# A two-layer decoder trunk: the second layer's output projection as seven half-size products inside one attention loop, split weights kept in DRAM, silu computed from tanh

## The chip, the cores and the metric

The kernel runs on one core of a Trainium2 chip. A core has five engines that run side by side, each with its own instruction queue: PE (TensorE, matrix products into PSUM), DVE (VectorE), ACT (ScalarE), POOL (GpSimd) and SP (SyncE, which here only issues DMA transfers). The metric is the device time of one execution in microseconds; lower is better.

## The reference

The input is `x` of 1024 tokens by 1024 channels, float32. Layer A is a chunked gated MLP. Layer B is sliding-window attention over a shared K/V. What matters here is layer B:

```python
q, z = jnp.split(h @ w_in, 2, axis=-1)            # (1024, 1024) each
...
logits = jnp.einsum('btkgd,bskd->bkgts', qb, kb) + alibi   # blocks of 128 tokens, window 128
...
y = out * jax.nn.silu(z)
return y @ w_out                                   # (1024, 1024) @ (1024, 1024)
```

There are 16 query heads of 64 channels on 4 K/V heads. The layer's result is rms-normalised, multiplied by a gain and added to the residual stream. The inputs of the products are float32.

## The kernel before

**Products.** Every float32 operand is split into a high part in the `fp32r` format and the rest (`split`, lines 104-110: ACT makes the high part, DVE the rest), and a product is three matmuls, high by high, high by low, low by high (`mm3`, lines 168-171). One matmul of 128 x 128 stationary values moves 512 columns.

**Layer A** (lines 298-930) already uses seven products for eight in its large matrix products, and is not touched. It ends at about 650 us.

**Layer B, first stage** (lines 1261-1276): `q_phase`, `kv_phase` and `z_phase` of the first 512 tokens (h = 0), while `chain_a` and `norm_h1` finish layer A's second half beside them, one generator step at a time. The weights come in tiles of 128 x 1024 (0.5 MB) in the order of `Weights.order` (line 120): 8 tiles of q, 4 of k/v, 8 of z, then 4, 8 and 8 again for the second 512 tokens, then 8 of the output projection. For each tile `wload` issues one transfer on SP into one of three `raw` buffers, and `split` or `split_scaled` writes the pair (`whi`, `wlo`, two buffers each). `wnext` hands out a pair and lets `ahead` split the next one and load one two further on. So each of the 20 tiles of q, k/v and z is read and split twice.

**Layer B, attention.** A `Unit` is one block of 128 tokens (b = 0 to 7) for one half of the heads (p = 0, 1). Its parts: `scores(0)` and `scores(1)` (PE 8 small matmuls each; DVE merges the window and finds the maximum; ACT takes EXP with the sum), `normalise` (DVE), `transposes` (PE 8, ACT two copies, POOL two triangular selections), `values` (PE, then ACT copy, DVE add, DVE product with the gate z, and the split of the result into the place of q). `attn` (lines 1163-1187) runs the 8 units of one half of the tokens as a software pipeline, unit i's scores beside unit i-1's transposes and unit i-2's values, in 10 rounds, and between these parts it takes steps of `fill`, a generator of other products: in the first loop k/v, q and half of z of the second tokens, in the second the rest of z and the output projection. A step is 6 matmuls of 512 columns, or about as much. Both loops run through to their ends one after the other (lines 1278-1289).

**Layer B, output.** `out_b0` (the first 512 tokens) holds four token tiles in PSUM for each half of the output columns (gd = 0, 1) and takes 8 k-tiles; `out_b1` does the second 512 tokens with split weights of a whole half in `big`, one token tile after the other, with `final` (sum of squares, power on POOL, two DVE passes, two stores) for each tile. `wo_b[gd, cp]` is the block of 256 rows (cp) and 512 columns (gd) of `w_out`.

**silu** is an ACT copy out of PSUM for each bank and one ACT SILU over two tiles (`z_phase`, lines 1010-1016).

**Order.** The program is written in Python and put in order by a scheduler that keeps each engine's instructions mostly as written and may move some by modelled times. PSUM has eight banks, four of tag `mm` and four of tag `s`.

## Time and profile before

| | |
|---|---|
| Three runs | 1056.62, 1056.23, 1053.37 us; median 1056.23 |
| The profiled execution | 1056.17 us, span 1054.5 us |
| Mean granted TensorE clock | 0.996 |
| HBM read, written | 125.28 MB, 31.46 MB |
| First attention score | about 768 us |
| Last matmul starts | 1047.77 us |

Times inside the span are in us from its start. "PE busy" is the union of the matmuls' durations, and a matmul's duration (0.39 us for 512 columns) is longer than the distance to the next one, so short gaps don't show in it. "PEld" is the loading of stationary values. A group's row gives line, engine, operation, tiles written and read, shapes and count; then busy us and mean ns; then the engine's idle time before it and what ended that. In the table by windows a row gives the stretch, its length, the busy times of PE, PEld, DVE, ACT and POOL with counts, the granted clock, the DMA share and GB/s.

### The profile page before, as it was taken

Reading aid. Unit: us, or ns where it says so; the run is one execution under the profiler, and the core shown is the slowest. Engines: PE = TensorE matmul, PEld = TensorE weight load, DVE = VectorE, ACT = ScalarE, POOL = GpSimd, SP = SyncE. Lnnn points to the kernel's source line nnn. Section 1 sums busy time; section 2 is a strip of 40 time slices with the busy share of each in tenths; the row PEclk is TensorE's granted clock in tenths of the full one; section 3 lists DMA queues with packets and bytes.
Section 4 is the critical chain, followed back from the end, with each engine's and each line's share of the span. In section 5 each row is a group of like instructions: output and inputs, shape, how many; then the busy total and the mean of one; then the engine's idle time right before and its main releaser. Section 6 shows DMA issues by size and latency. Waiting matters only on the chain.

```text
span 1054.5 us, 13950 instructions
## 1 busy us (share of the span) xinstructions
PE 1038.2 (98%) x5106; PEld 856.0 (81%) x5106; DVE 738.4 (70%) x1259; ACT 588.1 (56%) x1012; POOL 186.9 (18%) x153
## 2 busy tenths in 40 slices
PE   9999999999999999999999999999999999989997
PEld 7888888888888888888888888888898777867676
DVE  6987466867767768678596587764258885668763
ACT  6584443555565555555444474654467776686531
POOL 0000003254343542540200000100001011011120
PEclk9999999999999999999999999999999999999899
DMA  8777252334333433337997543632322122212363
GB/s 306 266 271 285 100 180 83 123 112 136 120 115 115 151 105 135 110 131 279 327 342 271 190 148 95 214 106 80 100 80 62 51 70 80 81 40 81 100 216 123
DMA packets 81508, 157.64 MB, mean 149 GB/s; under 512 B 5920, under 2 KB 33440, under 8 KB 81440
## 3 DMA queue, kind: packets, MB, share of 16 engines
q1 hardware_dynamic: 76928, 148.08, 41.1%
q10 hardware_dynamic: 4512, 8.68, 2.3%
q8 instruction: 40, 0.66, 0.2%
q14 instruction: 28, 0.23, 0.1%
HBM read 125.28 MB, written 31.46 MB: 149 GB/s over the span
## 4 chain that ended last, share of the span: by engine, by line
PE 83%; DVE 6%; ACT 5%; DMA 3%; issue 2%; POOL 1%; SPq 0%; DVEq 0%; POOLq 0%; ACTq 0%
PE ub L169 6%; PE ub L171 6%; PE ub L170 6%; PE ob L169 5%; PE qz L169 5%; PE ob L171 5%; PE ob L170 5%; PE qz L171 4%; PE qz L170 4%; PE uc L170 3%; PE uc L169 3%; PE uc L171 3%; PE sp L624 3%; PE oc L169 2%; PE oc L171 2%; PE oc L170 2%
## 5 line engine op out<-in xcount | busy, mean ns | idle before, releaser
L169 PE MATMUL qz<-n_hi,whi 128*128 128x512 f32 x256 | 101.6, 397 | 1.0 <-DVE q_lo L1004 0.8
L110 DVE SCALAR_TENSOR_TENSOR wlo<-raw_w,gn,whi 128x512 fp32r<-128x512 f32 x80 | 58.3, 759 | 61.3 <-ACT whi L109 61.1
L171 PE MATMUL qz<-n_hi,wlo 128*128 128x512 f32 x256 | 100.0, 391 | 0.3 <-DVE wlo L110 0.3
L170 PE MATMUL qz<-n_lo,whi 128*128 128x512 f32 x256 | 99.9, 390 | 0.0
L109 ACT ACTIVATE whi<-raw_w,gn 128x512 fp32r<-128x512 f32 x80 | 54.4, 715 | 53.6 <-PE qz L170 33.4
L1110 ACT ACTIVATE pr<-pr,mx 128x129 f32<-128x129 f32 x128 | 50.3, 395 | 38.3 <-DVE mx L1106 38.1
L169 PEld LDWEIGHTS qz<-n_hi,whi 128*128 128x128 f32 x256 | 48.1, 188 | 15.7 <-issue 6.2
L105 ACT ACTIVATE uzhilo_g<-f 128x1024 fp32r<-128x1024 f32 x31 | 32.9, 1061 | 49.5 <-PE uc L171 43.5
L171 PEld LDWEIGHTS qz<-n_hi,wlo 128*128 128x128 f32 x256 | 48.0, 188 | 11.1 <-DVE wlo L110 0.7
L170 PEld LDWEIGHTS qz<-n_lo,whi 128*128 128x128 f32 x256 | 48.1, 188 | 9.2
L106 DVE TENSOR_TENSOR uzhilo_g<-f,uzhilo_g 128x1024 fp32r<-128x1024 f32 x31 | 38.6, 1246 | 19.9 <-ACT uzhilo_g L105 19.9
L209 ACT ACTIVATE uz_slots<-ub 128x512 f32<-128x512 f32 x48 | 28.3, 590 | 42.4 <-PE ub L171 39.1
L169 PE MATMUL ub<-T,whi_g 128*128 128x512 f32 x128 | 50.7, 396 | 0.0
L169 PE MATMUL ub<-T,uzhilo_g 128*128 128x512 f32 x128 | 50.5, 395 | 0.0
L171 PE MATMUL ub<-T,wlo_g 128*128 128x512 f32 x128 | 49.9, 390 | 0.0
L171 PE MATMUL ub<-T,uzhilo_g 128*128 128x512 f32 x128 | 49.9, 390 | 0.0
L170 PE MATMUL ub<-T,whi_g 128*128 128x512 f32 x128 | 49.9, 389 | 0.0
L170 PE MATMUL ub<-T,uzhilo_g 128*128 128x512 f32 x128 | 49.8, 389 | 0.0
L169 PE MATMUL uc<-T,uzhilo_g 128*128 128x512 f32 x124 | 48.9, 395 | 0.0
L170 PE MATMUL uc<-T,uzhilo_g 128*128 128x512 f32 x124 | 48.3, 390 | 0.0
L171 PE MATMUL uc<-T,uzhilo_g 128*128 128x512 f32 x124 | 48.3, 389 | 0.0
L105 ACT ACTIVATE whi_g<-raw_uz 128x1024 fp32r<-128x1024 f32 (+1 forms) x31 | 26.5, 854 | 37.0 <-PE ua L170 14.5
(337 smaller groups left out, 3103.4 us busy)
## 6 DMA issues: line engine op xcount, KB each, us to landing
raw_uz<-in_wuz_in_dram SPq DMA_DIRECT2D x32, 512.0 KB, 3.5
raw_w<-in_wqz_dram SPq DMA_DIRECT2D x32, 512.0 KB, 3.5
td<-uz_slots SPq DMA_DIRECT2D x56, 256.0 KB, 2.1
orawP2a<-td SPq DMA_DIRECT2D x28, 512.0 KB, 4.1
raw<-in_wv_in_dram SPq DMA_DIRECT2D x17, 512.0 KB, 4.9
vg<-vd SPq DMA_DIRECT2D x8, 1024.0 KB, 5.4
orawP2b<-in_wo_a_dram SPq DMA_DIRECT2D x16, 512.0 KB, 8.2
vraw<-in_wv_in_dram SPq DMA_DIRECT2D x13, 512.0 KB, 5.2
```

The lines of the kernel that those rows point to most:

```text
L105: nc.scalar.activation(hi, src, AF.Copy)
L106: nc.vector.tensor_tensor(lo, src, hi.bitcast(F32), ALU.subtract)
L109: nc.scalar.activation(hi, src, AF.Copy, scale=g)
L110: nc.vector.scalar_tensor_tensor(lo, src, g, hi.bitcast(F32), ALU.mult, ALU.subtract)
L169: nc.tensor.matmul(out, lhsT=a_hi, rhs=b_hi, start=start, stop=False, skip_group_check=True)
L170: nc.tensor.matmul(out, lhsT=a_hi, rhs=b_lo, start=False, stop=False, skip_group_check=True)
L171: nc.tensor.matmul(out, lhsT=a_lo, rhs=b_hi, start=False, stop=stop, skip_group_check=True)
L209: nc.scalar.activation(out, a, AF.Copy)
L624: nc.tensor.matmul(psv[:, n], lhsT=d["vg"][:, 4 * j + n, i * P:(i + 1) * P], rhs=d["wc"], start=True, stop=True)
L1110: nc.scalar.activation(pr[:, i], pr[:, i], AF.Exp, bias=mx[:, i:i + 1], scale=-1.0, accum_out=dn[:, i:i + 1])
```

## The change

Write the gated attention output as A (1024 x 1024) and `w_out` as B, both cut in four. The output's four quarters were eight products of half size. Now they are seven, with sums on both sides (a Strassen-Winograd scheme):

- *Sums of B* (`presum`): per 512-column piece four loads, four additions or subtractions on POOL and four stores to DRAM (`sd[1]` to `sd[4]`), one generator step at a time beside q, k/v and z of the first tokens.
- *Sums of A* are made in `Unit.values`: results of the first tokens are stored to DRAM as well (`yd`), read again (`y_again`) for the units of the second tokens, and added on POOL (the last unit's on DVE); the sums' splits go into places of q0 and q1 that are free by then.
- *Three products in the loop* (`Out.early`): two accumulate in one bank set to the first quarter of the output, the third uses a sum. *Four products after it* (`Out.late`), each 4 token tiles x 4 k-tiles, with the additions between quarters on DVE and POOL, and `final` for each tile in the last two.
- *Kept weights*: when one of the first 20 tiles is split, its pair is stored to DRAM; the next 20 entries of the order read the pairs back (two transfers of 0.5 MB) instead of loading and splitting. In that stretch the pairs rotate through three places, the third made of two `raw` buffers, and are read two ahead.
- *One loop* over the 16 units with a written order of parts and filling (`ORDER`), the steps dealt out by round: 88 over the first 14 rounds, then 4 in each of the last 4. `held` chains the DVE and ACT instructions of the attention's parts in program order. `normalise` works on four heads at a time.
- *silu from tanh*: z (1 + tanh(z/2)) is twice silu(z); ACT takes TANH out of PSUM, DVE adds one and multiplies by PSUM, and the factor 0.5 goes into the copy after the transposes.

The core of the diff:

```diff
     def split(self, i):
...
-                hi = wpool.tile([P, 1024], F32R, tag="whi", name=f"whi{n}")
-                lo = wpool.tile([P, 1024], F32R, tag="wlo", name=f"wlo{n}")
+                hi, lo = (w_ring.take if 20 <= n < 40 else w_pair)(f"w{n}")
+                self.done.append((hi, lo))
+                if kind in self.kept:
+                    for t, src in zip((hi, lo), self.kept[kind]):
+                        nc.sync.dma_start(out=t.bitcast(F32), in_=src)
+                    continue
...
+                self.kept[kind] = [dram.tile([P, 1024], F32, name=f"kept{n}_{i}") for i in range(2)]
+                for t, dst in zip((hi, lo), self.kept[kind]):
+                    nc.sync.dma_start(out=dst, in_=t.bitcast(F32))
...
         def ahead(self):
-            self.split(self.at)
+            self.split(self.at + (20 <= self.at < 39))
             self.load(self.at + 2)
...
-            zt = z[m // 4]
-            nc.scalar.activation(zt[:, m % 4], ps, AF.Copy)
-            if m % 2 == 1:
-                zs = zt[:, m % 4 - 1:m % 4 + 1]
-                nc.scalar.activation(zs, zs, AF.Silu)
+            zt = z[m // 4][:, m % 4]
+            nc.scalar.activation(zt, ps, AF.Tanh, scale=0.5)
+            nc.vector.scalar_tensor_tensor(zt, zt, 1.0, ps, ALU.add, ALU.mult)
...
+            if b < 4:
+                hi, lo = (by_head(w)[:, 2 * p:2 * p + 2, t] for w in q)
+                split(hi, lo, yt.rearrange("p (m g) t -> p m g t", m=2))
+                nc.sync.dma_start(out=yd[p][t].rearrange("p (a t) -> p a t", a=4), in_=yt)
+            elif p == 0:
+                d = y_again(0, t)
+                add(mixed(d), yt, mixed(d), ALU.subtract, nc.gpsimd)
+                put(q, 0, d)
+            else:
+                hi, lo = (by_head(w)[:, 2:4, t] for w in q)
+                split(hi, lo, yt.rearrange("p (m g) t -> p m g t", m=2))
+                e = z[0][:, :, bs_]
+                eng = nc.gpsimd if t < 3 else nc.vector
+                add(e, yt, e, ALU.subtract, eng)
+                add(yt, e, mixed(y_again(0, t)), ALU.add, eng)
+                hi, lo = (by_head(w)[:, 0:2, t] for w in q0)
+                split(hi, lo, yt.rearrange("p (m g) t -> p m g t", m=2))
...
+    ORDER = "0F1FvtnmFF"
...
+    def presum():
+        for u in range(2):
+            for j in range(2):
+                cs = slice(j * 512, j * 512 + 512)
+                two = [bp.tile([P, 1088], F32, tag="pr", name=f"presum{u}{j}{i}", bufs=2) for i in range(2)]
+                a11, a21, a22, a12 = (two[i][:, k * 512:k * 512 + 512] for i in range(2) for k in range(2))
+                for t, (gd, cp) in ((a21, (1, u)), (a22, (1, 2 + u)), (a11, (0, u)), (a12, (0, 2 + u))):
+                    load(t, wo_b[gd, cp][:, cs])
+                yield from range(4)
+                made = ((1, a22, a21, a22, ALU.add), (3, a21, a11, a21, ALU.subtract),
+                        (2, a11, a22, a11, ALU.subtract), (4, a12, a12, a11, ALU.subtract))
+                for i, t, l, r, op in made:
+                    add(t, l, r, op, nc.gpsimd)
+                    yield
+                yield from range(3)
+                for i, t, *_ in made:
+                    nc.sync.dma_start(out=sd[i][u][:, cs], in_=t)
+                yield from range(7)
...
+        def late(self):
...
+            ps = [bank("mm", f"oe{t}") for t in range(4)]
+            for t in range(4):
+                for m in range(4):
+                    self.mm(ps[t], q0, 0, t, m, self.w6, m == 0, m == 3)
+                operand(q0, 1, t, t7[:, :, t * P:(t + 1) * P])
+                add(m1[t], m1[t], ps[t], ALU.add)
+                add(m5[t], m5[t], m1[t], ALU.add, nc.gpsimd)
...
+            ps = [bank("mm", f"og{t}") for t in range(4)]
+            for t in range(4):
+                for m in range(4):
+                    self.mm(ps[t], q1, 1, t, m, w3, m == 0, m == 3)
+                c = yo[t][:, 0:512]
+                add(c, m5[t], ps[t], ALU.add)
+                sumsq(ss[1][:, 0, t:t + 1], c, f"c12_{t}")
+                add(c, c, gp[:, 0:512], ALU.mult)
+                final(1, t, [c, yo[t][:, right]], ss[1])
...
-    main = q_phase(0, n0, q0)
+    main = q_phase(0, n0, q0, 0, 4)
+    sums = presum()
     step(main, main)
     for _ in main:
         step(side)
+        step(sums)
...
-    fill = chain(kv_phase(1, n1), q_phase(1, n1, q1), z_phase(1, n1, z1, 0, 4))
-    attn(0, q0, z0, fill, 64)
+    last = Out(q0, q1, gp, z1)
+    fill = chain(kv_phase(1, n1), q_phase(1, n1, q1, 0), z_phase(1, n1, z1, 0, 4), q_phase(1, n1, q1, 4),
+                 z_phase(1, n1, z1, 4, 8), last.early())
+    units = [Unit(4 * h + b, p, q, z) for h, q, z in ((0, q0, z0), (1, q1, z1)) for p in range(2) for b in range(4)]
+    attn(units, fill, [int(88 * (i + 1) / 14) for i in range(14)] + [92, 96, 100, 104])
     drain(fill)
-
-    def tail():
...
-    fill = chain(z_phase(1, n1, z1, 4, 8), tail())
-    attn(1, q1, z1, fill, 48, 2)
-    drain(fill)
+    last.late_weights()
+    last.late()
```

More of the change, by code (lines that the diff above doesn't have):

```diff
@@ L1164, in attn, with more @@
+    def attn(units, fill, by):
         taken = [0, 0]
[L1165 to L1169 removed]
+        def more(i, k):
+            lo, hi = by[i - 1] if i else 0, by[i]
+            while taken[1] < lo + (hi - lo) * (k + 1) // 4:
                 taken[1] += 1
                 step(fill)
[L1173 removed]
@@ new lines, in attn @@
+            live, mid, old = i < len(units), 0 <= i - 1 < len(units), 0 <= i - 2
+            f = iter(range(4))
+            for what in ORDER:
+                if what == "F":
+                    held(more, i, next(f))
+                elif what == "0" and live:
+                    held(units[i].scores, 0)
+                elif what == "1" and live:
+                    held(units[i].scores, 1)
+                elif what == "v" and old:
+                    held(units[i - 2].values)
+                elif what == "t" and mid:
+                    held(units[i - 1].transposes)
+                elif what == "n" and live:
+                    held(units[i].normalise, 0)
+                elif what == "m" and live:
+                    held(units[i].normalise, 1)
@@ new lines, in tile_yoco, with held @@
+    PINS, UP = (), ("DVE", "Activation")
+    ORDER = "0F1FvtnmFF"
+    behind = {}
+    def held(what, *args):
+        start = len(nc.cur_bb.bb.instructions)
+        what(*args)
+        for ins in list(nc.cur_bb.bb.instructions)[start:]:
+            e = str(ins.engine).split('.')[-1]
+            if e in PINS or what.__name__ != "more" and e in UP:
+                if e in behind:
+                    tc.add_manual_dep(ins, behind[e], mybir.DependencyInfo(
+                        mybir.DependencyClass.NoSync, mybir.DependencyReason.DATA), reason="held")
+                behind[e] = ins.name
```

233 lines of the change are left out of this document (131 added, 102 removed).

## The prediction, as it was put on record

> **What bounds the kernel now.** I read the page first, then the table by windows, then the groups by line, then the chain that ended last. On the page the profiled execution has this span and these shares:
>
> ```profile
> span 1054.5 us, 13950 instructions
> PE 1038.2 (98%) x5106; PEld 856.0 (81%) x5106; DVE 738.4 (70%) x1259; ACT 588.1 (56%) x1012; POOL 186.9 (18%) x153
> DMA  8777252334333433337997543632322122212363
> ```
>
> TensorE is busy almost throughout, DVE and ACT are not, and the transfers are light behind the middle of the span. Up to about 650 us (layer A) the change touches nothing. The windows of layer B, with two stretches of layer A for the rate of the transfers:
>
> ```profile
> 520.00:540.00 20.00, 20.00 (x89) 16.54 (x89) 18.37 (x17) 8.94 (x10) 0.00 (x0) 1.00 1.05 387
> 0.00:50.00 50.00, 48.17 (x209) 39.12 (x210) 40.35 (x46) 31.72 (x43) 1.42 (x6) 1.00 0.82 289
> 650.00:700.00 50.00, 49.69 (x221) 40.79 (x220) 33.87 (x49) 27.92 (x47) 3.82 (x3) 1.00 0.52 177
> 700.00:768.00 68.00, 68.00 (x363) 58.71 (x363) 29.45 (x43) 31.92 (x52) 0.00 (x0) 1.00 0.29 93
> 768.00:860.00 92.00, 91.09 (x562) 74.91 (x561) 72.42 (x213) 64.42 (x177) 10.92 (x10) 1.00 0.21 66
> 860.00:1048.00 188.00, 181.93 (x969) 142.23 (x967) 122.27 (x320) 108.03 (x270) 28.37 (x27) 0.98 0.30 100
> ```
>
> The columns are PE, PEld, DVE, ACT and POOL busy, granted clock, DMA share and GB/s. From 650 to 768 us (q, k/v and z of the first half) PE is full and the transfers run at 93 to 177 GB/s. From 768 to 1048 us (attention and output projection) PE has gaps, and the clock falls to 0.98 in the mean.
>
> A busy PE hides gaps shorter than a matmul, so I count that last stage. The spacing of back-to-back 512-column matmuls comes from twelve of them, the first and the last here; the price of the attention's parts from merged pieces of the chain; the counts from groups by line between 767.8 and 1048 us:
>
> ```profile
> 1045.27 0.39 PE L169 MATMUL ob<-wob_hi,q_hi 128*128 128x512 f32 x1
> ...
> 1047.77 0.39 PE L171 MATMUL ob<-wob_hi,q_lo 128*128 128x512 f32 x1
> ```
>
> ```profile
> 784.84 0.87 PE pt L1123 x8
> 785.71 0.87 PE s L1092 x8
> 857.94 1.45 PE o L1152 x16
> 985.12 0.43 PE ob L171
> ```
>
> ```profile
> L169 PE MATMUL qz<-n_hi,whi 128*128 128x512 f32 x128 | 51.8, 405 | 1.0 <-DVE q_lo L1004 0.8
> L169 PE MATMUL ob<-whi,q_hi 128*128 128x512 f32 x64 | 26.8, 419 | 0.1
> L169 PE MATMUL ob<-wob_hi,q_hi 128*128 128x512 f32 x64 | 25.1, 393 | 0.0
> L169 PE MATMUL pv<-whi,n_hi 128*128 128x256 f32 x32 | 9.1, 286 | 0.0
> L169 PE MATMUL pk<-n_hi,whi 128*128 128x512 f32 x16 | 6.5, 404 | 0.0
> ```
>
> Spacing: 2.50 us over 11 steps, 0.227 us. Each group stands for three (lines 169 to 171). So q and z: 384 x 0.227 = 87.2; output projection, 3 x (64 + 64) = 384: 87.2; k: 48 x 0.227 = 10.9; v at half the columns, 96 x 0.114 = 10.9; sixteen attention units at 2 x 0.87 (scores) + 0.87 (transposes) + 1.45 (values) = 4.06: 65.0. Sum 261 us of work in 280 us. **About 19 us are lost here**, of which some 3.5 are the clock: matmuls 0.43 us apart near 985 us, and 188 x 0.02 = 3.8. The rest are waits at the ends of the two attention loops and between: the chain runs there over ACT, DVE and POOL.
>
> **The change, part by part.**
>
> *Seven products for eight.* A product of half size is 4 token tiles x 4 k-tiles x 3 = 48 matmuls; eight were 384, seven are 336. Removed: 48 x 0.227 = **10.9 us** of PE work, in the stage where PE is the bound. No attention, q, k, v or z matmul changes.
>
> *One loop and a fixed order.* 18 rounds instead of 20, no emptied loop between, and 88 of the 104 filling steps spread over the first 14 rounds: 6.3 steps x 6 matmuls x 0.227 = 8.6 us of filling beside 4.06 of attention, 12.6 us a round. Values wait for what was transposed one round before. What the other engines must do in that round:
>
> ```profile
> L1106 DVE CUSTOM_DVE_ANT_0 pr<-s,bias,snk 128x128 f32<-128x128 f32 x128 | 39.0, 349 | 1.5
> L110 DVE SCALAR_TENSOR_TENSOR wlo<-raw_w,gn,whi 128x512 fp32r<-128x512 f32 x38 | 28.1, 770 | 18.0 <-ACT whi L109 18.0
> L1110 ACT ACTIVATE pr<-pr,mx 128x129 f32<-128x129 f32 x128 | 50.3, 395 | 38.3 <-DVE mx L1106 38.1
> L109 ACT ACTIVATE whi<-raw_w,gn 128x512 fp32r<-128x512 f32 x38 | 25.6, 712 | 3.0 <-PE pv L171 1.1 <-ACT pr L1110 1.0 <-ACT pc L1125 0.6
> L1110 ACT ACT_TABLE_LOAD x4 | 5.1, 1283 | 0.0
> L1016 ACT ACT_TABLE_LOAD x3 | 3.8, 1283 | 0.1
> ```
>
> Reading split weights back takes the splits out of the loop: 28 us off DVE, 26 off ACT, of the 195 and 172 us that the two windows from 768 us give. Both stay well below PE, so this is worth only the waits that it ends. In exchange the loop reads 1.05 MB a tile for 0.52 and moves y and C11 pieces through DRAM, some 10.5 + 6 MB over about 210 us (104 x 1.36 + 65), 80 GB/s beside the 66 to 100 of the windows: hidden. On SP a pair's load waits for PE to leave its slot, with those pieces queued behind it; three pairs in the ring give them two tiles of time. Of the 19 lost us I expect 6 to stay (short waits where PSUM banks change hands between the three products in the loop, and in the last two rounds, which have only 4 steps each): **13 us gained**; bounds 2 (only the end of the first loop) and 17.
>
> *silu from tanh.* ACT loses the SILU passes and gets a tanh for a copy of the same tile; DVE gets 16 products of 512 columns, some 0.69 each (the L754 row below is the nearest). Both lie under PE. Whether tanh and exp share a table no row shows: the nearest rows are the seven loads above, one at each change of function. At one per change that is up to 16 x 1.28 = 20 us of ACT, less than the 26 that the splits leave free (about 1 us of PE, which lies in the 6 above; I take it); at none, 0. The Trainium skill (ScalarE: Activation LUTs, Table sets: the hidden batching unit) lists tanh in the set anchored by exp, so by it the loads vanish; no run here shows it, and the sum by it would be 1 us lower.
>
> *Kept weights and presums: the price.* While PE does q, k/v and z of the first half, SP's queue now also stores 20 pairs (2 x 0.52 MB each, 21.0 MB) and moves 16 loads and 16 stores of 0.26 MB for the sums (8.4 MB); the first pairs of the loop are read there instead of raw tiles (about 1.6 MB more). Before, the stretch moved 177 x 50 + 93 x 68 = 15.2 MB. Together 46 MB in 118 us. The best sustained rate on show, 387 GB/s at a share of 1.05, gives 119 us; so the transfers become as long as the matmuls. It is uneven: the first 50 us ask for 8.9 + 8 pairs (8.4) + half the sums (4.2) = 21.5 MB, 55.5 us; the next 68 for 24.7 MB, 64 us. What hides it are the two slots of each weight half and the reads ahead:
>
> ```profile
> L109 ACT ACTIVATE whi<-raw_w,gn 128x512 fp32r<-128x512 f32 x39 | 26.7, 717 | 43.3 <-PE qz L170 33.4 <-PE pv L171 8.5 <-issue 1.3
> raw_w<-in_wqz_dram SPq DMA_DIRECT2D x32, 512.0 KB, 3.5
> h1d<-yoa SPq DMA_DIRECT2D x8, 512.0 KB, 2.9
> ```
>
> Today a split waits for PE to leave its slot, 33 us in all; a tile takes PE 24 x 0.227 = 5.5 us and its split some 2.2, so 3.3 us per tile are free, and a slot's store has 11 - 2.2 = 8.9 us to land where an unloaded one lands in 2.9. The stores queue behind splits on SP, and the loads of later raw tiles behind the stores; PE would wait for those. I take **5 us lost**: the first 50 us are over by 5.5, of which stores may lag a little, and the first pair of the loop comes late by about 1. Bounds: 0 if the lag is all hidden; 15 at the rate that the first window suggests (289 / 0.82 = 352 GB/s: 46 MB take 131 us).
>
> The Trainium skill (DMA: Bandwidth & Descriptors, Specifications) speaks against this part: it names about 358 GB/s as one core's share of HBM. By it 46 MB take 128 us and the loss would be about 11 us. The window at 387 GB/s does not agree with that as a limit.
>
> *Work on GpSimd.* Sums of 128x512 cost POOL this, and a DVE add with SBUF operands is sometimes stretched:
>
> ```profile
> L206 POOL TENSOR_TENSOR f<-raw_uz x15: 1284/1292/1995, 158.7 to 449.5; 128x512 f32<-128x512 f32 x15
> L206 DVE TENSOR_TENSOR uz_slots<-uz_slots x8: 680/688/1350, 193.3 to 497.9; 128x512 f32<-128x512 f32 x8
> ```
>
> 16 presums, 20.7 us where POOL did 3.8 us in the windows from 650 us: hidden. In the loop two more adds per late unit: hidden, unless a select queues behind them in the last rounds (in the 6).
>
> *The end.* Four products, 4 x 10.9 us, run alone with DVE:
>
> ```profile
> L754 DVE TENSOR_TENSOR yb<-ob,gpb 128x512 f32<-128x512 f32 x7 | 4.8, 692 | 13.9 <-ACT junk_ob L183 13.9
> L106 DVE TENSOR_TENSOR wob_lo<-raw_ob,wob_hi 128x1024 fp32r<-128x1024 f32 x8 | 9.7, 1231 | 4.7 <-ACT wob_hi L105 4.7
> L1229 DVE SCALAR_TENSOR_TENSOR yb<-yb,ef,hf 128x512 f32<-128x512 f32 x10 | 7.2, 748 | 2.5 <-POOL ef L1221 2.2 <-DMA hf<-h1d 0.3
> L1220 DVE TENSOR_SCALAR ef<-ssb,ef 128x1 f32<-128x1 f32 x7 | 1.4, 208 | 0.1
> ```
>
> DVE: 8 splits of weights (9.8), 8 of operands and 16 adds and 4 gains at 0.69 (19.3), 16 last products (12.0), 16 small ones (2.9): 44 us in 44. In the last product each tile costs DVE 0.69 + 0.69 + 0.36 + 1.50 = 3.24 against PE's 2.73; after four tiles it is 1.5 behind, and an add now stands ahead of the sum of squares, 0.69. **2.5 us more** behind the last matmul; bounds 0.7 and 8 (if DVE starts the last product behind).
>
> **Sum** against the profiled execution (1056.17 us, 1.7 more than its span; the median is 1056.23): 1056.2 - 10.9 - 13 + 5 + 2.5 = **1040 us**.
>
> **Rivals.**
> - *A: transfers wholly hidden and gaps nearly closed.* For: 33 us of slack at the splits. 1056.2 - 10.9 - 16 + 0 + 1 = 1030.
> - *B: DVE bounds the end.* For: 44 of 44 us and POOL adds beside them. 1040 + 8 = 1048.
> - *C: the fixed order waits in turn.* ACT and DVE stand still for a late value and everything behind it waits; the 2 us bound holds instead of 13: 1040 + 11 = 1051, or, with a few more us where banks change hands, up to 1057. Against: DVE keeps 195 - 28 = 167 us of work for some 250.
> - *D, slower: the stores hold the slots.* A split now waits for its slot's two stores as well as for PE. If they land later than 8.9 us, a tile takes (2.2 + landing) / 2 instead of 5.5. The gain is gone when 20 tiles lose 21 us (the 16 of the forecast and the 5 counted in it): 6.6 us a tile, a landing of 11. With two pairs, a raw tile and four pieces of the sums ahead (3.7 MB, 9.6 us at 387 GB/s, and 2.9) it is 12.5: 7.3 us a tile, 20 x 1.8 = 36 us, 1040 - 5 + 36 = 1071. Against: such bursts come four times in the stretch, not for every tile.
> - *E: a lower rate.* If the stretch runs at the 352 GB/s of the first window's row, 46 MB take 131 us for 118: 13 lost instead of 5, 1048. For: small pieces and both directions mixed. Against: the 387 row. The page's 358 GB/s would give 1046.
>
> **How the numbers follow.** Forecast 0.43, A 0.18, B 0.12, C 0.10, D 0.10, E 0.07. The forecast's own bounds are 1033 to 1047. 1029 to 1054 leaves out D, a part of C and the ends. Over 0.3% (some 3 us, about what a measurement of this kernel can tell from no change) faster: forecast, A, B, E and 0.02 of C, 0.82; within it 0.05 (C); slower 0.13 (D and the rest of C).
>
> **What would show it.** 336 output-projection matmuls and no gain on them elsewhere; from 650 us to the first score, DMA share near 1 and 118 to 128 us; a loop without half-clock matmuls and of about 210 us; a DVE without idle time in the last 44 us. Wrong if the stretch before the loop grows by over 15 us (D), if the loop keeps over 12 us of gaps (C), or if the last matmul is followed by over 12 us.

## The result and the profile after

The kernel after takes 1107.26 us (median of four runs, 1106.32 to 1109.91) beside 1056.07 us for the kernel before: ratio 1.049 (interval 1.047 to 1.052). **The change costs 51 us; the forecast was a gain of 16, and the time lies above the whole range and above every rival.** The profiled execution has a span of 1104.6 us for 1054.5. First the page of the kernel after:

```profile
span 1104.6 us, 14153 instructions
...
PE 1057.8 (96%) x5058; PEld 849.4 (77%) x5058; DVE 765.8 (69%) x1287; ACT 556.9 (50%) x976; POOL 254.5 (23%) x195
...
DMA  8786243342333333367985617989854343321647
```

There are 48 matmuls fewer (5058 for 5106), as forecast, and yet TensorE is busy 20 us longer. The transfers are dense in the middle now, and POOL works 68 us more. The windows of layer B in the kernel after (length; PE, PEld, DVE, ACT, POOL; clock, DMA share, GB/s):

```profile
668.30:800.40 132.10, 122.72 (x590) 99.62 (x589) 73.77 (x114) 58.30 (x105) 26.23 (x19) 0.99 0.89 321
800.40:1038.20 237.80, 222.36 (x1260) 170.14 (x1262) 165.21 (x471) 121.56 (x366) 55.38 (x40) 0.98 0.37 124
1034.50:1087.00 52.50, 48.20 (x208) 37.39 (x208) 36.69 (x46) 19.79 (x37) 29.63 (x22) 0.97 0.56 177
1087.00:1104.60 17.60, 0.19 (x1) 0.00 (x0) 10.89 (x24) 2.17 (x6) 2.19 (x4) 0.61 0.78 264
```

Layer B now starts at 668 us instead of 654, although nothing of layer A was changed; and behind the last matmul stand 17.6 us in which DVE works 10.9.

To see where the time went I cut the span at five marks: the first matmul of q, the first one of the second tokens' k (the attention begins there), the last one of `values`, the last matmul, and the end. "Lost" is the length less the matmuls in it at 0.227 us for 512 columns (the prediction's way of counting):

| stage | before: length, lost | after: length, lost |
|---|---|---|
| layer A | 654.2, 7.3 | 668.3, 21.4 |
| q, k/v, z of the first tokens | 114.5, 0.5 | 132.1, 15.8 |
| attention with its filling | 240.8, 17.5 | 237.8, 32.6 |
| products after it | 38.3, 0.3 | 48.6, 5.8 |
| behind the last matmul | 6.7, 6.5 | 17.8, 17.6 |

The losses grow by 14.1, 15.3, 15.1, 5.5 and 11.1 us, 61 together; the seven products take 11 back, and 50 remain. (Where a stage begins and ends can shift a part of about 1 us from one to the next; the sum stays.) The experiments take these five one by one.

### The profile page after: what moved, and what is told of

Its sections match the earlier page's. It is cut to its first block, busy times and chain, and to the rows that moved or that the text cites. A ratio compares the mean times of both kernels' runs of the same rounds, so it can differ in the third digit from the quotient of the medians.

```text
span 1104.6 us, 14153 instructions
## 1 busy us (share of the span) xinstructions
PE 1057.8 (96%) x5058; PEld 849.4 (77%) x5058; DVE 765.8 (69%) x1287; ACT 556.9 (50%) x976; POOL 254.5 (23%) x195
## 4 chain that ended last, share of the span: by engine, by line
PE 79%; DVE 10%; DMA 3%; ACT 3%; issue 2%; POOL 2%; SPq 0%; DVEq 0%; ACTq 0%; POOLq 0%
PE ub L194 5%; PE ub L195 5%; PE ub L196 5%; PE qz L194 4%; PE qz L196 4%; PE qz L195 4%; PE uc L194 3%; PE uc L195 3%; PE uc L196 3%; PE ob L194 3%; PE ob L196 3%; PE ob L195 3%; PE sp L635 3%; PE vb L195 3%; PE vb L196 3%; PE vb L194 2%
## 5 line engine op out<-in xcount | busy, mean ns | idle before, releaser
L196 PE MATMUL qz<-n_hi,wlo_w 128*128 128x512 f32 x216 | 86.9, 405 | 5.1 <-DVE wlo_w L110 5.1
L194 PE MATMUL qz<-n_hi,whi_w 128*128 128x512 f32 x216 | 88.5, 410 | 2.7 <-ACT whi_w L109 2.0
L195 PE MATMUL qz<-n_lo,whi_w 128*128 128x512 f32 x216 | 87.0, 403 | 0.0
L196 PEld LDWEIGHTS qz<-n_hi,wlo_w 128*128 128x128 f32 x216 | 41.5, 192 | 17.4 <-DVE wlo_w L110 7.5
L110 DVE SCALAR_TENSOR_TENSOR wlo_w<-raw_w,gn,whi_w 128x512 fp32r<-128x512 f32 x40 | 34.0, 884 | 29.4 <-ACT whi_w L109 29.3
L194 PEld LDWEIGHTS qz<-n_hi,whi_w 128*128 128x128 f32 x216 | 41.9, 194 | 12.4 <-ACT whi_w L109 2.6
L231 POOL TENSOR_TENSOR f<-raw_uz 128x512 f32<-128x512 f32 x15 | 20.0, 1335 | 130.5 <-DMA raw_uz<-in_wuz_in_dram 87.3
L231 POOL TENSOR_TENSOR f<-raw_uz,raw_uz 128x512 f32<-128x512 f32 x15 | 19.2, 1282 | 132.8 <-DVE uzhilo_g L106 132.8
L195 PEld LDWEIGHTS qz<-n_lo,whi_w 128*128 128x128 f32 x216 | 41.8, 193 | 9.0
```

Source lines behind the costliest of these rows:

```text
L110: nc.vector.scalar_tensor_tensor(lo, src, g, hi.bitcast(F32), ALU.mult, ALU.subtract)
L194: nc.tensor.matmul(out, lhsT=a_hi, rhs=b_hi, start=start, stop=False, skip_group_check=True)
L195: nc.tensor.matmul(out, lhsT=a_hi, rhs=b_lo, start=False, stop=False, skip_group_check=True)
L196: nc.tensor.matmul(out, lhsT=a_lo, rhs=b_hi, start=False, stop=stop, skip_group_check=True)
L231: (eng or nc.vector).tensor_tensor(out, a, b, op)
```

## The experiments

All ratios are to runs of the kernel before on the same chip, which took 1054.2 to 1055.4 us (medians).

### Layer A: where the buffers lie

The matmuls of layer A are further apart from the first microsecond on. One and the same window, kernel before and then after:

```profile
100.00:400.00 300.00, 299.60 (x1406) 250.40 (x1405) 210.22 (x304) 158.36 (x195) 96.93 (x73) 1.00 0.37 125
```

```profile
100.00:400.00 300.00, 299.69 (x1375) 244.69 (x1374) 201.79 (x296) 151.81 (x187) 95.97 (x73) 1.00 0.36 121
```

PE is full and the clock 1.00 in both, but 1375 matmuls were done for 1406. Singly, after's are 0.233 us apart:

```profile
99.44 0.39 PE L194 MATMUL vc<-whi,T 128*128 128x512 f32 x1
...
102.94 0.40 PE L194 MATMUL vc<-vhi,T 128*128 128x512 f32 x1
```

That is 3.50 us over 15 steps. What differs is one line of `Out`: two tiles of 32 bytes in the pool `const` where the kernel before had one.

```diff
+            self.ss = [const.tile([P, 2, 4], F32, name=f"ssb{h}") for h in range(2)]
```

All pools behind `const` (the weights' `wpool` and all others but `big`, which is opened ahead of it) therefore start 32 bytes further in each partition. Two runs shift them by an unused tile:

```diff
+    pad = const.tile([P, 8], F32, name="pad")
+    nc.vector.memset(pad, 0.0)
```

**e1_before_plus32**, the kernel before with it:

> The kernel before, with one unused tile of 32 bytes per partition more in its constants' pool (and one memset of it), so that every later SBUF pool starts 32 bytes further on, as it does in the changed kernel. Theory (placement): the matmuls' spacing, 227 ns in the kernel before and 233 in the changed one from the first microseconds on, follows from operands that no longer start on a multiple of 64 bytes; then this kernel's spacing goes to 233 and its time to about 1082 (4000 matmuls of 512 columns x 6.3 ns, and a little for the shorter ones). Rival (something of the changed program as a whole, its length, instruction fetch or DMA traffic): spacing 227, time 1056.

Measured 1072.6 us, 1.017 (1.016 to 1.019), 18.2 us more than the kernel before; layer A ends at 668.0, spacing 233.3 ns. The place alone makes this.

**e2_after_plus32**, the kernel after with it (64 bytes off):

> The changed kernel with the same 32-byte tile, so that the pools lie on multiples of 64 bytes again. Theory (placement): spacing back to 227 ns, some 26 us gained, about 1081; the other 25 us of the loss stay and belong to the stages of layer B. Rival: spacing stays 233 and the time 1107.

Measured 1102.9, 1.046 (1.045 to 1.048): spacing 229 ns in parts of layer A and 233 in others. That 64 bytes would restore the speed was wrong. **e17_before_plus128** asks for 128 (`[P, 32]`):

> The kernel before with a tile of 128 bytes that nothing uses in the pool `const`, so that all later pools lie 128 bytes further (with 32 bytes it takes 1072.6, matmuls 233 ns apart for 227; with 64 the spacing is 229 to 233). If what counts is the place within 128 bytes: spacing 227, total 1054 to 1056. If it is the place as such, or within a larger unit: 229 or more, over 1060.

Measured 1069.6, 1.014 (1.011 to 1.016), spacing 232.4 ns. So it isn't the place within 128 bytes either. **e5_in_place** takes the cause away in the kernel after:

```diff
-            self.ss = [const.tile([P, 2, 4], F32, name=f"ssb{h}") for h in range(2)]
+            self.ss = [pool.tile([P, 2, 4], F32, name=f"ssb{h}") for h, pool in enumerate((const, bp))]
```

> The changed kernel with one of its two small sum tiles (32 bytes) taken from the last SBUF pool instead of the constants' pool, so that every pool starts where it does in the kernel before. Nothing else differs. Theory (the spacing depends on where the operands lie, and it is their whole place that counts, since a shift by 64 bytes brought only 4 us): spacing 227 ns, layer A's end back from 668 to 654 us, the time about 1090. Rival (the changed program itself is slower on PE): spacing stays at 229 to 233 and the time at 1100 or more.

Measured 1090.6, 1.034 (1.032 to 1.036), and the window is as before the change, with 1410 matmuls:

```profile
100.00:400.00 300.00, 299.70 (x1410) 250.74 (x1409) 209.46 (x303) 158.92 (x196) 97.42 (x74) 1.00 0.36 123
```

**16.7 of the 51 us are the place of the buffers.** The other stages lose what they lost (14.8, 33.7, 5.4 and 18.0 us), so e5 is the base of what follows, except for e3 and e4, whose base is e2.

### The stage before the loop: stores, or sums of the weights

**e3_no_kept** leaves the kept weights out (no stores; raw tiles read and split again):

```diff
-                hi, lo = (w_ring.take if 20 <= n < 40 else w_pair)(f"w{n}")
+                hi, lo = w_pair(f"w{n}")
...
-                for t, dst in zip((hi, lo), self.kept[kind]):
-                    nc.sync.dma_start(out=dst, in_=t.bitcast(F32))
```

> As the previous kernel, but the split weights are not stored to and read from DRAM: the second use loads and splits again, as before the change. Theory (the stores hold the slots and PE waits for splits from the first q product to the second half's k): that stretch returns from about 130 us to about 116, and the loop loses at most 5 us to the 54 us of splits that come back to ACT and DVE: 1070 to 1075. Rival (the waits there come from the presums on POOL and their transfers, not from the stores): the stretch stays above 124 and the time is 1081 or more.

Measured 1108.6, 1.051 (1.049 to 1.053): the stage loses 8.3 us for 16.4, but the loop 47.4 for 33.8. I had expected the loop to mind little; in this loop the kept weights pay for themselves. **e7_no_presum** leaves the sums of the output weights out:

```diff
-    sums = presum()
+    sums = iter(())
```

> As e5, but the sums of the weight quarters are left out: the four late products and the third in the loop use plain quarters of the weights, so that 16 loads, 16 additions on POOL and 16 stores beside q, k/v and z of the first tokens are gone. Theory (in that stretch half of the lost 16 us come from the presums: their transfers, and DVE's splits that run slower while POOL adds): the stretch from the first q product to the second half's k shortens from about 131 to 122 us, and the time by 8 to 9 us. Rival (the kept pairs' stores alone hold the slots): less than 4 us.

Measured 1077.7, 1.022 (1.020 to 1.025), 12.9 below e5. With stores alone the stage loses 2.5 us, with sums alone 8.3 (e3; some 1.6 of it the wider spacing, as e2's 16.4 stand to e5's 14.8), with both 14.8. Beside the 0.5 of the kernel before that is about 2 for the stores, 6 for the sums and 14 for both, so the two prices don't add. ACT's waits in this stage say where they meet, in e5 and then in e7:

```profile
ACT whi_w L109 <- DMA raw_w<-in_wqz_dram: 23.8, 7, 6.4
```

```profile
ACT whi_w L109 <- DMA raw_w<-in_wqz_dram: 8.2, 2, 6.1
```

The splits wait for raw tiles that come late; before the change none of this line's waits is put down to a load (its row is in the prediction). The time from issue to landing in e5, first of the raw tiles and then of the kept pairs:

```profile
DMA to landing us min/median/max: 4.9/7.1/8.6
```

```profile
DMA to landing us min/median/max: 2.6/5.2/7.9
```

In the kernel before a raw tile lands in 3.5 us in the median. No split is seen to wait for a kept store. **e10_presum_no_add** drops only the additions:

```diff
                 for i, t, l, r, op in made:
-                    add(t, l, r, op, nc.gpsimd)
                     yield
```

> The kernel after with the buffers in place (1090.6), without the sixteen additions on POOL that form the sums of the output weights; their loads and stores stay (so four of the seven products use a plain quarter of the weights, and the output is another). Leaving out the sums whole took the stretch before the loop from 131 to 116.5 us. Theory 1, POOL's additions stretch DVE's splits (from 750 to about 880 ns) and so PE waits: the stretch falls to 118 to 121, total 1078 to 1081. Theory 2, the sums' 8.4 MB of transfers beside the stores of the kept weights delay the raw tiles: it stays at 128 to 131, total 1088 to 1091.

Measured 1083.2, 1.026 (1.024 to 1.029); the stage, 131.1 us in e5, takes 126.4. First its window in e7, then in e10:

```profile
653.50:770.00 116.50, 114.17 (x570) 96.66 (x568) 62.51 (x91) 54.44 (x91) 3.81 (x3) 1.00 0.84 301
```

```profile
653.60:780.00 126.40, 121.02 (x590) 101.09 (x589) 67.40 (x114) 58.36 (x105) 3.81 (x3) 0.97 0.93 338
```

So both theories hold a part: of the 14.6 us by which this stage differs between e5 and e7, 4.7 are the additions and 9.9 the transfers (42.7 MB: 126.4 x 338), the lower clock of 0.97 in e10 included. Without the additions ACT still waits 22.1 us for raw tiles. How an addition on POOL reaches DVE shows in the split's durations (min/median/max), after and then e10:

```profile
L110 DVE SCALAR_TENSOR_TENSOR wlo_w<-raw_w,gn,whi_w x36: 737/750/1864, 679.3 to 788.3; 128x512 fp32r<-128x512 f32 x36
```

```profile
L110 DVE SCALAR_TENSOR_TENSOR wlo_w<-raw_w,gn,whi_w x36: 743/748/754, 660.4 to 768.9; 128x512 fp32r<-128x512 f32 x36
```

Without additions no split takes over 754 ns; with them some take up to 1864, 1.1 us more, and an addition itself takes 1.29. The Trainium skill (SBUF — State Buffer, Who interferes with whom) says that a DVE instruction with two SBUF inputs contends with a GpSimd instruction that reads SBUF, and that this contention is an exclusive lock. If a split that meets an addition waits for its end, it is longer by up to one addition; the trace agrees.

### The loop

**e4_no_fixed_order**, the chaining of the attention's DVE and ACT instructions (`held`) off:

```diff
-    PINS, UP = (), ("DVE", "Activation")
+    PINS, UP = (), ()
```

> As the changed kernel on multiples of 64 bytes, but DVE's and ACT's instructions of the attention are not chained in program order; the scheduler may order them. Theory (the fixed order makes ACT and DVE wait in turn and costs the loop's gaps): the loop, 251 us before this, gets shorter by 5 to 12 us. Rival (the gaps come from too little filling and from changes of PSUM banks, whatever the order): same within 3 us, or slower since the scheduler's own order is worse.

Measured 1100.2, 1.043 (1.041 to 1.046), 2.7 below e2 in all: not the main cause. In the loop several rounds are as forecast (12.5 to 12.6 us long, under 0.5 lost); the losses stand in a few others. One is that at 926 us, in the kernel after. PE's timeline has the scores:

```profile
925.75 0.25 PE L1101 MATMUL s<-kh,q_hi 128*128 128x192 f32 x1
```

DVE's timeline, until their merge begins:

```profile
925.21 1.37 DVE L1126 TENSOR_TENSOR pr<-pr,dn 128x512 f32<-128x512 f32 x1
926.51 1.06 DVE L1080 COPY pr<-snk 128x8 f32<-128x8 f32 x1
927.58 0.74 DVE L1015 SCALAR_TENSOR_TENSOR q_hi<-qz,qsc,q_hi 64x512 fp32r<-64x512 f32 x1
...
929.88 0.76 DVE L1015 SCALAR_TENSOR_TENSOR q_lo<-qz,qsc,q_lo 64x512 fp32r<-64x512 f32 x1
930.67 0.30 DVE L1108 COPY_PREDICATED s<-mrg,s 128x128 f32<-128x128 uint32 x1
```

The merge starts 4.9 us after the scores, because DVE first finishes two stretched instructions (1.37 us for 0.69 in the median of this line, and 1.06 for 0.16 at the shortest) and four that empty q's banks. `values` and the transposes stand behind the maximum (`mx`) that follows. PE's waits in the loop, kernel after (total, times, longest):

```profile
PE pt L1133 <- DVE mx L1115: 5.0, 6, 2.3
PE od L194 <- DVE raw_c L1334: 2.5, 2, 2.0
PE s L1101 <- ACT pc L1135: 2.4, 1, 2.4
```

**e6_values_first** puts the values ahead of the first filling:

```diff
-    ORDER = "0F1FvtnmFF"
+    ORDER = "0vFFt1nmFF"
```

> As the previous kernel with another order in each round: scores of the first heads, values, two fillings, transposes, scores of the second heads, normalisation, two fillings (the order of the kernel before), instead of scores, filling, scores, filling, values, transposes. Theory (values and transposes take the four PSUM banks that the scores have just filled, so PE waits each round until DVE has read them, and DVE comes late because it first empties the fillings' banks in turn): with values ahead of any wait for the second scores, 8 to 15 us less than the previous kernel. Rival (DVE is simply late in every order, slowed by POOL): within 4 us of it.

Measured 1085.4, 1.030 (1.028 to 1.032); the loop's loss falls from 33.7 to 29.1. Much of the rest lies in the last rounds, where the sums of A are made. On e6, **e15_no_y_sums** leaves them out:

```diff
-                d = y_again(0, t)
-                add(mixed(d), yt, mixed(d), ALU.subtract, nc.gpsimd)
-                put(q, 0, d)
+                hi, lo = (by_head(w)[:, 0:2, t] for w in q)
+                split(hi, lo, yt.rearrange("p (m g) t -> p m g t", m=2))
...
-                add(e, yt, e, ALU.subtract, eng)
-                add(yt, e, mixed(y_again(0, t)), ALU.add, eng)
```

> The kernel of e6_values_first (1085.4; buffers in place, values ahead of the first filling) without the sums of A in the loop: the units of the second tokens split their own results and read and add nothing (so four late products take plain or stale quarters of A, and the output is another). Theory that these sums (seven additions on POOL and one on DVE, eight reads from DRAM, four more splits) cause what the last rounds lose: the loop's 26 lost us fall by 8 to 10, total 1075 to 1078. Rival, the last four rounds lose because they have only four filling steps each: within 3 us, 1082 to 1086.

(By the code the sums are ten additions on POOL and two on DVE, not seven and one.) Measured 1070.5, 1.014 (1.011 to 1.018): 15.0 less, more than I expected; the loop loses 15.5. **e16_even_steps** then deals the steps evenly:

```diff
-    attn(units, fill, [int(88 * (i + 1) / 14) for i in range(14)] + [92, 96, 100, 104])
+    attn(units, fill, [int(104 * (i + 1) / 18) for i in range(18)])
```

> The kernel of e15_no_y_sums with the 104 filling steps dealt evenly over the 18 rounds (5.8 each) instead of 88 over the first 14 and 4 in each of the last; that is possible there because nothing is written over the first tokens' operands. Theory that a round with four steps (5.4 us of filling beside 4.1 of attention) is too short for its own chain of scores, exponentials, transposes and values: the loop loses 6 to 9 us less than e15. Rival, the sums alone: within 2 us of e15.

Measured 1063.3, 1.008 (1.006 to 1.011): 7.2 less. The loop's windows in e6, e15 and e16:

```profile
785.80:1017.30 231.50, 216.14 (x1249) 169.88 (x1251) 148.77 (x468) 118.96 (x358) 46.83 (x40) 0.97 0.36 124
```

```profile
786.50:1002.30 215.80, 208.44 (x1244) 164.79 (x1241) 145.29 (x466) 118.10 (x356) 33.07 (x30) 0.99 0.36 124
```

```profile
785.80:993.60 207.80, 204.91 (x1227) 161.21 (x1225) 144.63 (x465) 116.50 (x354) 33.58 (x30) 0.99 0.36 125
```

Lost are 29.1, 15.5 and 11.1 us. The dealing belongs to the sums: their splits are written over q0, so the products that read q0 must be done before the last rounds, which are left with too little filling.

### Behind the last matmul

In the third product after the loop, DVE does this for a tile (kernel after, DVE's timeline):

```profile
1074.32 0.68 DVE L231 TENSOR_TENSOR m<-m,of 128x512 f32<-128x512 f32 x1
1074.92 0.14 DVE L1243 TENSOR_SCALAR ef<-ssb 128x1 f32<-128x1 f32 x1
1075.86 0.21 DVE L1244 TENSOR_SCALAR ef<-ssb,ef 128x1 f32<-128x1 f32 x1 [0.79 <-ACT junk_c L208]
1077.76 0.75 DVE L1253 SCALAR_TENSOR_TENSOR raw_c11b<-raw_c11b,ef,hf 128x512 f32<-128x512 f32 x1 [1.69 <-POOL ef L1245]
1078.42 0.75 DVE L1253 SCALAR_TENSOR_TENSOR m<-m,ef,hf 128x512 f32<-128x512 f32 x1
1079.09 0.68 DVE L231 TENSOR_TENSOR m<-m,of 128x512 f32<-128x512 f32 x1
```

From this addition, the second tile's, to the third's 4.77 us pass, for the 2.73 that PE needs; DVE stands idle in half of it, waiting for the sum of squares and then for the power on POOL. POOL's timeline shows why that is late:

```profile
1075.90 1.30 POOL L231 TENSOR_TENSOR m<-m,gpb 128x512 f32<-128x512 f32 x1 [2.94 <-ACT junk_c L208]
1077.14 0.58 POOL L1245 TENSOR_TENSOR ef<-ef,small 128x1 f32<-128x1 f32 x1
```

The gain's multiplication stands ahead of it. DVE carries the lag into the last product. There the last matmul of the first tile and that of the last tile start at

```profile
1078.64 0.39 PE L196 MATMUL og<-s,q_lo 128*128 128x512 f32 x1
...
1086.80 0.39 PE L196 MATMUL og<-s,q_lo 128*128 128x512 f32 x1
```

and their additions at

```profile
1084.98 0.67 DVE L231 TENSOR_TENSOR yb<-m,og 128x512 f32<-128x512 f32 x1
...
1095.00 0.68 DVE L231 TENSOR_TENSOR yb<-m,og 128x512 f32<-128x512 f32 x1
```

that is 6.3 and 8.2 us later. The chain at the end also names the residual tiles, which come through two buffers. Three runs: **e8_finals_behind** does each closing one tile later, so that the power has time.

```diff
-                final(0, t, [r, c], ss[0])
+                if held_back:
+                    final(*held_back, rs)
+                held_back = (0, t, [r, c], ss[0])
```

> As e5, but in the last two products the two closing passes of a token tile come after the additions of the next tile, so that DVE doesn't stand still for POOL's power in between. Theory (8 tiles go through one chain of add, sum of squares, power and two passes, 4.8 us a tile in the last but one product and 3.5 in the last, against 2.7 of PE; DVE waits in order): the 17.8 us behind the last matmul fall to about 10, 7 to 8 us gained. Rival (DVE and POOL are full in this stage, order or not): 2 us or less.

Measured 1089.7, 1.034 (1.032 to 1.036): the end stays at 17.9. **e9_late_loads_ahead** also loads the residual tiles early:

```diff
+                hx[0, t] = wpool.tile([P, D], F32, tag=("whi", "wlo")[t % 2], name=f"hx0{t}")
+                load(hx[0, t], h1d[0][t])
```

> The kernel after with the buffers in place and the finals one tile behind (1089.7), and the eight tiles of the residual stream that `final` needs are loaded into places that are free, ahead of all the stores of the last two products, instead of through two buffers one after the other. Theory that these loads, queued on SP behind stores that wait for their results, hold the 18 us behind the last matmul: they fall to 10 to 12, total 1082 to 1084. Rival, the two engines themselves (DVE with eight closings of some 3 us, and its two-operand additions stretched by POOL's): not more than 2 us, 1088 to 1090.

Measured 1092.0, 1.035 (1.033 to 1.037): no gain, though those loads are no longer in the chain. **e14_gain_on_dve** moves the multiplication, in the second and third product:

```diff
-                add(c, c, gp[:, right], ALU.mult, nc.gpsimd)
+                add(c, c, gp[:, right], ALU.mult)
```

> The kernel of e9_late_loads_ahead (1092.0; buffers in place, finals one tile behind, residual tiles loaded ahead) with the multiplication by the gain in the second and third late product moved from POOL to DVE, where the kernel before has it. In the third late product a tile takes 4.75 us, because the power that the closing needs stands behind the multiplication of 1.3 to 1.8 us on POOL. Theory that this queue on POOL sets the pace and its lag is carried past the last matmul: a tile takes 3.5 to 3.8 us, the time behind the last matmul falls from 18 to 12 to 14, total 1086 to 1088. Rival, DVE's own work sets the pace (it gets eight more passes of 0.69): 18 us stay, or 1 to 2 more, 1091 to 1094.

Measured 1086.7, 1.030 (1.025 to 1.035): 13.8 us are lost behind the last matmul for 18.3 in e9, as the theory had it. DVE's timeline of e14 in the third product and then in the fourth:

```profile
1052.53 0.68 DVE L231 TENSOR_TENSOR m<-m,of 128x512 f32<-128x512 f32 x1
...
1054.80 0.68 DVE L231 TENSOR_TENSOR m<-m,of 128x512 f32<-128x512 f32 x1
...
1057.06 0.68 DVE L231 TENSOR_TENSOR m<-m,of 128x512 f32<-128x512 f32 x1
...
1070.55 0.68 DVE L231 TENSOR_TENSOR yb<-m,og 128x512 f32<-128x512 f32 x1
...
1074.08 0.68 DVE L231 TENSOR_TENSOR yb<-m,og 128x512 f32<-128x512 f32 x1
```

The third product starts with 2.27 us from addition to addition, less than PE's 2.73, but the fourth has 3.53.

### What is good in the change, and whether the prices add up

**e12_before_tanh** is the kernel before with silu from tanh only:

```diff
+            nc.scalar.activation(zt, ps, AF.Tanh, scale=0.5)
+            nc.vector.scalar_tensor_tensor(zt, zt, 1.0, ps, ALU.add, ALU.mult)
```

> The kernel before with silu from tanh alone. If tanh needs no table load of its own beside exp, the loads between z and exp in the loops go and ACT's 16 copies and 8 SILU passes become 16 passes; PE waits for ACT at few places only: 2 to 5 us less, 1049 to 1052. If ACT is hidden at all these places: no difference, within 1 us. If each change between tanh and exp loads a table: up to 5 us more.

Measured 1051.7, 0.996 (0.995 to 0.998). In its attention a single table load is left for before's seven (L1110 and L1016 in the prediction):

```profile
L1014 DVE SCALAR_TENSOR_TENSOR z<-z,qz 128x512 f32<-128x512 f32 x9 | 6.1, 682 | 1.4 <-ACT z L1013 1.3
...
L1108 ACT ACT_TABLE_LOAD x1 | 1.3, 1283 | 0.0
```

The Trainium skill (ScalarE: Activation LUTs, Table sets: the hidden batching unit) has tanh in exp's set; this trace agrees. **e13_before_kept_tanh** adds the kept weights:

```diff
+                hi, lo = (w_ring.take if 20 <= n < 40 else w_pair)(f"w{n}")
...
+                for t, dst in zip((hi, lo), self.kept[kind]):
+                    nc.sync.dma_start(out=dst, in_=t.bitcast(F32))
```

> The kernel before with the kept weights (pairs stored to DRAM, read back for the second tokens, three places) and silu from tanh, with the eight products, the two attention loops and the end of before, and no sums. From the kernel without sums (stretch 116.5, 2.5 lost) and the kernel without kept weights (loop 16 us longer): the stretch before the loop grows by 2 us, the loops shrink by 5 to 10: 1046 to 1052. If the waits that the kept weights ended were those of the one-loop order alone, before's loops stay as they are and the total is 1056 to 1058.

Measured 1051.6, 0.997 (0.996 to 0.998). The stage loses 2.2 us, the loops 10.6 (tanh alone: 12.2), so the kept weights about break even with two loops. **e18_no_sums** is e16 with e7's and e14's edits: the seven products without their sums.

> The kernel of e16_even_steps (1063.3; no sums of A in the loop, steps dealt evenly) also without the sums of the output weights (as in e7_no_presum) and with the late gains on DVE, the closings one tile behind and the residual tiles loaded ahead (as in e14_gain_on_dve): seven products with kept weights and tanh, but hardly any of what they need beside their matmuls, and another output. If the single prices add up (12.9 for the sums of the weights, 3.8 for the late end): 1046.6, so 1044 to 1049, at last below the kernel before. If they overlap (each took away waits that another would have covered): 1050 to 1056.

Measured 1050.1, 0.995 (0.993 to 0.997). Beside e13, which has eight products and the same kept weights and tanh, the last matmul comes 11.6 us sooner after the end of the first stage (260.5 us for 272.1), about what 48 matmuls are worth, and the time behind the last matmul is 9.1 us longer (15.7 for 6.6). **e19_first_and_gain** is e14 with e6's order:

> The change whole, with its buffers in place, values ahead of the first filling (as in e6_values_first, 1085.4) and the late end of e14_gain_on_dve (3.8 us less than the kernel in place): 1080 to 1083 if the two add up; not below the kernel before in any case, since the sums and the dealing of the steps stay.

Measured 1084.3, 1.028 (1.025 to 1.031), only 1.1 below e6, with 18.2 us behind the last matmul: the two cures don't add up, and nothing that keeps the seven products whole comes near the kernel before. The versions that beat it, e12 and e13, keep the eight.

## Why the prediction was wrong, point by point

- **"Up to about 650 us (layer A) the change touches nothing": failed, 14.1 us there and 16.7 in all.** No instruction of layer A changed, but the place of its operands did. e1 and e5 show it from both sides. No rival of mine had this term; without it the result (1090.6) would still lie above all of them.
- **Seven for eight, 10.9 us: right.** 5058 matmuls for 5106; e18 beside e13 has the gain in the matmul stages whole.
- **"One loop and a fixed order", 13 us gained: failed; 15 us were lost.** The steady rounds are as predicted. Rival C's chaining is worth 2.7 us (e4). What I passed over with "hidden, unless a select queues behind them" are the sums of A, which I put at nothing: 13.6 us of the loop's loss, and 4.4 for the uneven dealing they force (e15, e16). Another 4.6 come from the place of the values in the order (e6). What is left, 11.1, is what e13 loses with two loops (10.6): one loop by itself gains nothing over two once kept weights and tanh are in.
- **Splits out of the loop, "worth only the waits that it ends": too low.** In this loop the splits would cost 13.6 us more (e3).
- **silu from tanh, a cost of 0 to 1 us: wrong in sign**; a gain of 3.7 in the kernel before (e12).
- **Kept weights and presums, 5 us lost, bound 15: mis-sized.** 15.3. The mechanism was the one forecast, raw tiles that land late behind the other transfers (e5's waits above). Rival D's falls, although its sign, a stage longer by over 15 us (17.6 here), appeared: the kept pairs land within 7.9 us, inside D's 8.9, and no split is seen to wait for their stores. The stores alone cost 2 us (e7), the sums alone about 6 (e3), both about 14; what the sums add to the stores is 9.9 us by their transfers and 4.7 by POOL's additions (e10), which I had put at nothing. My 46 MB were about right (42.7), the 387 GB/s were not a rate to be held: the stage runs at 321 to 338. Kernel after, at its best:

```profile
700.00:720.00 20.00, 16.83 (x64) 13.13 (x65) 8.16 (x13) 5.87 (x10) 3.70 (x3) 0.91 1.03 392
```

  The Trainium skill (DMA: Bandwidth & Descriptors, Specifications) names about 358 GB/s as a core's limit of HBM. These 20 us run above it and the whole stage below it, so no run here shows it as a limit, though it lay nearer to the stage's rate than my 387.
- **"Work on GpSimd: hidden": failed.** POOL had the time, but its additions stretch DVE's instructions with two SBUF inputs: 4.7 us in the stage before the loop (e10).
- **The end, 2.5 us more, bound 8: failed; 11.1, and 5.5 in the late products.** I compared DVE with PE tile by tile only for the last product, with DVE's work at 3.24 us a tile, which was near the 3.53 measured; for the other three I only summed DVE's work (44 us in 44), and a sum has no waits in it. But the third product has four closings too, and DVE waits in them because the power queues behind a multiplication on POOL: its additions start 5.40, 4.77 and 1.66 us apart for PE's 2.73, and the last product begins on DVE 6.3 us behind PE. Rival B's place was right, not its price. e14 takes 4.5 of it away in one arrangement and e19 little in another, and without the sums of A in the loop 15.5 remain (e18), so how the rest divides between DVE's work and the late start of the third product's closings is open.

Each rival had one mechanism and the forecast's gains beside it; here four prices came together, and the largest (16.7 us in all) began in a stage that I had set aside.

## What to carry to other kernels

A fast matrix scheme pays with TensorE time for sums on other engines and queues: price the sums' additions, transfers and the order that they force, stage by stage, before counting the matmuls saved; here, apart from the buffers' place, 11 us saved came with 46 us lost (1104.6 - 14.6 - 1054.5 + 11; 14.6 is the span that e5 takes off), the one loop and the kept weights included. In a kernel bound by TensorE, look at the spacing of matmuls in an untouched stage first: a tile of 32 bytes in an early pool can move every later buffer and cost more than the change is worth (18.2 us in e1), so give new tiles a place behind what is tuned. For the end of a kernel, compare per tile what PE takes with the chain of the closing, POOL's queue included, for every product that closes and not just for the last.

## What the runs showed of the hardware that was not expected

- **The place of the operands in SBUF sets the pace of these matmuls.** 227 ns apart in the kernel before; with the pools behind `const` moved by 32 bytes 233.3, by 64 bytes 229 to 233, by 128 bytes 232.4, at a full clock. `big` did not move, so what counts may be where the operands lie to each other; no run here tells that, and the rule stays open.
- **Half clock follows the longer stops.** In the kernel after, the granted clock falls to 0.5 five times for 3.4 us, and once more behind the last matmul (0.986 in the mean). Ahead of each of the five PE had stood still for 1.9 to 2.6 us of 3.4. One of them, with the 3.4 us ahead of it:

```profile
934.00:937.40 3.40, 0.81 (x7) 0.47 (x5) 2.83 (x10) 2.70 (x7) 0.00 (x0) 1.00 0.05 19
937.40:940.80 3.40, 3.40 (x10) 2.85 (x11) 2.75 (x4) 1.46 (x7) 0.32 (x1) 0.50 0.02 5
```

  At half clock the five are worth 8.5 us of matmuls (5 x 3.4 / 2). The kernel before has one such stretch of 6.8 us ahead of its last matmul, e13 none (0.998). A stage's loss holds these stretches too, so a wait costs more than its own length. That the stop is the cause is read from the order in time; no run changes it alone.
- **A DVE instruction with two SBUF inputs beside a POOL addition** takes up to 1.86 us for 0.75, and the late splits of 128x1024 took 3.72 us for two in the kernel after, for 1.23 and 1.22 in e14, where the multiplications had left POOL.
